# Decay factors of two chunked mixers: masked differences of running sums by two products in the short float32 format, in place of one full float32 product

## The chip, the cores and the metric

The kernel runs on one core of one Trainium2 chip. The metric is the device time of one execution in microseconds (us); the median of the timed runs counts. TensorE (PE in the views, its weight loads are PEld) multiplies, VectorE (DVE) and ScalarE (ACT) work on tiles of 128 partitions, GpSimd (POOL) does a few powers, and SyncE (SP) issues the transfers.

## The reference, cut to what matters

Two layers, each of a SwiGLU feed-forward half step, a token mixer and a second feed-forward half step, on 256 tokens of 1024 features. The mixer runs three groups of heads side by side: differential attention, Mamba-2 (8 heads) and gated DeltaNet (4 heads). The last two need, for every head and every pair of tokens of a block, the factor by which a state decays between them:

```
def segsum_exp(a_cs):
    l = a_cs.shape[-1]
    tril = jnp.tril(jnp.ones((l, l), dtype=bool))
    diff = a_cs[..., :, None] - a_cs[..., None, :]
    return jnp.where(tril, jnp.exp(jnp.where(tril, diff, 0.0)), 0.0)
```

`a_cs` is the running sum of the log decays of a head. There are 12 heads and two blocks of 128 tokens, so 24 tables of 128 x 128 numbers in each layer.

## The kernel before, in words

Every large product is made in float32r, a float32 that the matrix engine multiplies in a shorter format. An operand is split into a high part (the ScalarE cast of line 250) and the rest (the VectorE subtraction of line 251), and three products replace one. Weights come in units of 128 x 1024 numbers; `load` brings them into a ring of 5 buffers, `split` splits them into rings of 7, and `job` (lines 301 to 364) multiplies: lines 327, 342, 343 and 345 for the first matrices and the input projection, lines 238, 239, 241 and 245 for the second matrices and the output projection. Small products, among them those of the decays, are full float32 and go through the helper `mm` (line 389). A full float32 product leaves two matmul records in the trace, a transpose (line 260) or a float32r product one.

In the mixer stage the input projection's units go on while "chains" (generators) turn its results into the three mixers: after each job, `step` advances those chains whose due time, in a clock that the program counts up by hand, has come. The order in which the generator emits instructions is only a first order: when the program is built, a scheduler puts each engine's queue in order by its own estimate of when operands are ready, so that instructions of a chain can stand between two products of one job.

`decays` (line 555) is such a chain. From the gate columns it computes `a12`, the log decays of 12 heads and two blocks (128 x 24), the running sums by two products with triangular constants (`csps`, lines 593 to 595), and then for each of three groups of four heads and each block: a VectorE product `ar` (line 605) of the log decays with the triangle `UT`, a full float32 product of 512 columns with the triangle `SL` (`dps`, line 613), and the exponential (`ex`, line 614). For the first group, which DeltaNet uses, line 618 multiplies the result by `UT` to clear the part above the diagonal; the Mamba groups are masked later through `CB`. The results go out as `E`: `delta` reads `E 0` in line 693 (`LA`), `after_m11` reads `E 1` and `E 2` in line 927.

Other chains that share the queues in this stretch: the attention's `aps`, `dops`, `do`, `dsq`, `dss`, `rsq` and the transposes `mTps` of its result; DeltaNet's `ssps`, the power `r` on GpSimd (line 660), `laps` and `LA`, and the triangular inverse (`gps`, `ups`); the convolutions `conv` of ScalarE and VectorE (lines 516 to 540). Small PSUM results share four banks (`aux`).

Of the kernel before, what the change touches and what calls it, by code (L numbers as in the profile page):

```python
# [10 lines left out]
F32 = mybir.dt.float32  # L11
F32R = mybir.dt.float32r
# [28 lines left out]
LEVELS = (2, 4, 8, 16, 32)  # L41
C_COS = C_LV + 32 * len(LEVELS)
C_SEL = C_COS + 2 * 16
C_N = C_SEL + 2

# [19 lines left out]
def constants():  # L67

    c = np.zeros((P, C_N), np.float32)
    i = np.arange(P)  # L70
    c[:, C_ID : C_ID + P] = np.eye(P)
    c[:, C_UT : C_UT + P] = i[:, None] <= i[None, :]
    c[:, C_SL : C_SL + P] = i[:, None] > i[None, :]

    r, q = i[:, None] % 64, np.arange(64)[None, :]
    c[:, C_M1 : C_M1 + 64] = -1.0 * ((r + 1 == q) & (r % 2 == 0))
    c[:, C_I64 : C_I64 + 64] = r == q
    for n, s in enumerate(LEVELS):
        cols = q[:, (q[0] // s) % 2 == 0]
        c[:, C_LV + 32 * n : C_LV + 32 * (n + 1)] = ((r // s) % 2 == 1) & (r // (2 * s) == cols // (2 * s))  # L80
    freq = np.float32(500000.0) ** (-np.arange(0, 8, 2, dtype=np.float32) / np.float32(8))
    ang = np.arange(SEQ, dtype=np.float32)[:, None] * freq[None, :]
    cos, sin = np.cos(ang), np.sin(ang)
    for b in range(2):
        r = slice(b * P, (b + 1) * P)
        at = C_COS + 16 * b
        c[:, at : at + 16] = np.concatenate([cos[r], cos[r], -sin[r], sin[r]], 1)
    c[:, C_SEL : C_SEL + 2] = i[:, None] // 64 == np.arange(2)[None, :]
    return c


class Kernel:
# [76 lines left out]
    def setup_late(self):  # L169

        nc, a = self.nc, self.a
        c = self.const
        nc.sync.dma_start(self.cst[:, P:], a["cst"][:, P:])
        yield 2

        def bc(name, n, *aps):
            t = c.tile([P, n], F32, name=name)
            at = 0
            for ap in aps:
                nc.sync.dma_start(t[:, at : at + ap.shape[0]], ap.partition_broadcast(P))  # L180
                at += ap.shape[0]
            return t

        self.bias12, self.nA, self.mD, self.nlam = ([] for _ in range(4))
        rows = c.tile([P, P], F32, name="convrows")

        nrows = c.tile([P, P], F32, name="normrows")
        nc.vector.memset(nrows, 0.0)
        for l in range(L):
            r0 = 64 * l  # L190
            nc.sync.dma_start(rows[r0 : r0 + 32], a["m_conv_w"][l].rearrange("k (t c) -> (k t) c", c=P))
            nc.sync.dma_start(rows[r0 + 32 : r0 + 40], a["m_conv_b"][l].rearrange("(t c) -> t c", c=P))
            nc.sync.dma_start(rows[r0 + 40 : r0 + 64], a["g_conv_w"][l].rearrange("k (t c) -> (k t) c", c=P))
            yield 2
            self.bias12.append(bc(f"bias12_{l}", 12, a["g_dt_bias"][l], a["m_dt_bias"][l]))
            self.nA.append(bc(f"nA_{l}", 12, a["g_A_log"][l], a["m_A_log"][l]))
            yield 2
            self.mD.append(bc(f"mD_{l}", 8, a["m_D"][l]))
            r0 = 6 * l
            nc.sync.dma_start(nrows[r0 : r0 + 4], a["m_norm_w"][l].rearrange("(t c) -> t c", c=P))  # L200
            for n, w in enumerate(("g_norm_w", "da_subln_w")):
                r = nrows[r0 + 4 + n : r0 + 5 + n]
                nc.sync.dma_start(r[:, 0:64], a[w][l : l + 1])
                nc.sync.dma_start(r[:, 64:P], a[w][l : l + 1])
            yield 2
        lp = bc("lamp", L * 4 * 32, a["da_lambda"].rearrange("l a b -> (l a b)"))
        lp = lp.rearrange("p (l a b) -> p l a b", l=L, a=4)
        yield 12
        ps = self.aux(0, "cwps")
        nc.tensor.transpose(ps[:, :P], rows, self.ident)  # L210
        nc.tensor.transpose(ps[:, P : 2 * P], nrows, self.ident)
        self.cw = c.tile([P, P], F32, name="cw")
        nc.vector.tensor_copy(self.cw, ps[:, :P])
        self.nw = c.tile([P, 6 * L], F32, name="nw")
        nc.vector.tensor_copy(self.nw, ps[:, P : P + 6 * L])
        for l in range(L):
            nc.scalar.activation(self.nA[l], self.nA[l], AF.Exp)
            nc.vector.tensor_scalar(self.nA[l], self.nA[l], -1.0, None, op0=ALU.mult)
            w = self.nw[:, 6 * l + 5 : 6 * l + 6]
            nc.vector.tensor_scalar(w, w, 1.0 - lambda_init(l), None, op0=ALU.mult)  # L220
            pr = self.s(0, 2, "lsum")
            for m in range(2):
                q = self.h(0, [32], "lq")
                nc.vector.tensor_mul(q, lp[:, l, 2 * m, :], lp[:, l, 2 * m + 1, :])
                nc.vector.tensor_reduce(pr[:, m : m + 1], q, axis=AX.X, op=ALU.add)
            e = self.s(0, 2, "lexp")
            nc.scalar.activation(e, pr, AF.Exp)
            lam = c.tile([P, 1], F32, name=f"lam_{l}")
            nc.vector.tensor_sub(lam, e[:, 0:1], e[:, 1:2])
            nc.vector.tensor_scalar(lam, lam, lambda_init(l), None, op0=ALU.add)  # L230
            self.nlam.append(lam)
# [323 lines left out]
    def decays(self, l, hv):  # L555

        nc = self.nc
        ve = nc.vector
        stt = ve.scalar_tensor_tensor
        two = lambda t: t.rearrange("p (b n) -> p b n", b=2)  # L560

        be = self.s(0, 8, "be")
        nc.scalar.activation(two(be), hv[:, :, 0:4], AF.Exp, scale=-1.0)
        u = self.s(0, 24, "u")
        ve.tensor_tensor(two(u), hv[:, :, 4:16], self.bias12[l].unsqueeze(1).to_broadcast([P, 2, 12]), op=ALU.add)
        e = self.s(0, 24, "e")
        nc.scalar.activation(e, u, AF.Abs)
        nc.scalar.activation(e, e, AF.Exp, scale=-1.0)
        ve.tensor_scalar(be, be, 1.0, None, op0=ALU.add)
        beta = self.s(0, 8, "beta")  # L570
        ve.reciprocal(beta, be)
        yield 0.5

        d = self.s(0, 24, "d")
        ve.tensor_scalar(d, e, 2.0, None, op0=ALU.add)
        ve.reciprocal(d, d)
        z = self.s(0, 24, "z")
        ve.tensor_mul(z, e, d)
        z2 = self.s(0, 24, "z2")
        ve.tensor_mul(z2, z, z)  # L580
        q = self.s(0, 24, "q")
        ve.tensor_scalar(q, z2, 1.0 / 17.0, None, op0=ALU.mult)
        for k in (15.0, 13.0, 11.0, 9.0, 7.0, 5.0, 3.0):
            stt(q, in0=q, scalar=1.0 / k, in1=z2, op0=ALU.add, op1=ALU.mult)
        stt(q, in0=q, scalar=1.0, in1=z, op0=ALU.add, op1=ALU.mult)
        ve.tensor_scalar(u, u, 0.0, None, op0=ALU.max)
        sp = self.s(0, 24, "sp")
        stt(sp, in0=q, scalar=2.0, in1=u, op0=ALU.mult, op1=ALU.add)
        a12 = self.s(0, 24, "a12")
        ve.tensor_tensor(two(a12), two(sp), self.nA[l].unsqueeze(1).to_broadcast([P, 2, 12]), op=ALU.mult)  # L590
        yield 7

        ps = self.aux(0, "csps")
        self.mm(ps[:, 0:24], lhsT=self.UT, rhs=a12)
        self.mm(ps[:, 24:48], lhsT=self.SL, rhs=a12)
        ecs = self.s(0, 48, "ecs")
        nc.scalar.activation(ecs, ps[:, 0:48], AF.Exp)
        self.mx.update(beta=beta, dt=two(sp)[:, :, 4:12], ecs=two(ecs[:, 0:24]), erev=two(ecs[:, 24:48]))

        for n in range(3):  # L600
            ex = self.big([2, 4, P], "ex")
            for b in range(2):
                r = self.w([4, P], "ar")
                at = 12 * b + 4 * n
                ve.tensor_tensor(
                    r,
                    a12[:, at : at + 4].unsqueeze(2).to_broadcast([P, 4, P]),
                    self.UT.unsqueeze(1).to_broadcast([P, 4, P]),
                    op=ALU.mult,
                )  # L610
                yield 0.7
                pd = self.aux(b, "dps")
                self.mm(pd, lhsT=self.SL, rhs=r.rearrange("p h l -> p (h l)"))
                nc.scalar.activation(ex[:, b].rearrange("p h l -> p (h l)"), pd, AF.Exp)
            yield 0.6
            if n == 0:
                e8 = ex.rearrange("p b h l -> p (b h) l")
                ve.tensor_tensor(e8, e8, self.UT.unsqueeze(1).to_broadcast([P, 8, P]), op=ALU.mult)
            self.mx["E", n] = ex

    def after_v(self, l, ps):
# [655 lines left out]
```

## Time and profile before

| what | value |
|---|---|
| timed runs | 1081.48, 1086.86, 1087.26 us; median 1086.86 us |
| profiled execution | 1085.23 us, span 1083.5 us, mean granted TensorE clock 0.991 |
| busy share of the span | PE 98%, PEld 83%, DVE 70%, ACT 56%, POOL 3% |
| data moved | 184.34 MB, mean 170 GB/s |

The span runs from the first to the last instruction; what lies around it in the profiled execution is 1.7 us. Times in rows are from the span's start. Layer 1's mixer stage lies at about 200 to 357 us, layer 2's at about 735 to 887 us. A matmul's recorded duration is longer than its share of the engine, since matmuls are pipelined: how fast they go is read from the starts of successive ones, or from the chain that ended last, which lists the advance.

### The profile page before, as it was taken

What the parts mean: (1) busy time and instruction counts of PE and PEld (TensorE: products, weight loads), DVE (VectorE), ACT (ScalarE), POOL (GpSimd) and SP (SyncE); (2) the same over time, 40 slices, a digit from 0 to 9 for tenths busy, and PEclk for the clock granted to TensorE, in tenths of its full rate; (3) what the DMA queues carried; (4) which work ended last, traced back from release to release, by engine and by line L of the source; (5) the groups of instructions that cost most, each with busy time, mean ns of one, the idle gap of its engine ahead of it and who ended that gap; (6) DMA issues with size and microseconds to landing.
All of it is one profiled execution on the core that took longest, in us unless ns stands there. A gap on an engine that the chain in (4) does not pass through costs nothing.

```text
span 1083.5 us, 17613 instructions
## 1 busy us (share of the span) xinstructions
PE 1056.8 (98%) x6354; PEld 898.4 (83%) x6354; DVE 754.7 (70%) x1550; ACT 605.2 (56%) x1292; POOL 32.0 (3%) x29
## 2 busy tenths in 40 slices
PE   8999999999999999999999999999989999999996
PEld 7888888787987788888878888887878878888885
DVE  5777754886776877774587777457967787777644
ACT  6687643487434566664356666446863445666540
POOL 0000000001001000000000000000010010000000
PEclk9999999998999999999999999999999999999999
DMA  9967664653234676666477666646512449666641
GB/s 274 294 180 208 191 192 143 176 157 97 60 105 145 199 216 190 195 189 195 142 222 211 190 194 191 191 105 194 177 47 72 145 132 264 181 183 187 194 136 39
DMA packets 221551, 184.34 MB, mean 170 GB/s; under 512 B 14608, under 2 KB 201368, under 8 KB 221464
## 3 DMA queue, kind: packets, MB, share of 16 engines
q1 hardware_dynamic: 221464, 183.22, 57.7%
q8 instruction: 50, 0.82, 0.3%
q14 instruction: 37, 0.30, 0.1%
HBM read 182.13 MB, written 1.05 MB: 169 GB/s over the span
## 4 chain that ended last, share of the span: by engine, by line
PE 85%; DVE 8%; issue 2%; DMA 2%; ACT 2%; POOL 1%; SPq 0%; DVEq 0%; POOLq 0%; ACTq 0%
PE ps L327 43%; PE po L238 7%; PE po L239 7%; PE po L245 7%; PE ps L345 4%; PE ps L343 4%; PE ps L342 4%; DVE wl L251 3%; DMA raw<-in_ffn_w_gu_dram 1%; PE ups L389 1%; PE gps L389 1%; POOL rsq L430 1%; PE xps L260 1%; PE yps L389 1%; PE vnps L389 1%
## 5 line engine op out<-in xcount | busy, mean ns | idle before, releaser
L251 DVE TENSOR_TENSOR wl<-raw,wh 128x512 fp32r<-128x512 f32 (+1 forms) x672 | 436.3, 681 | 195.2 <-ACT wh L250 188.4
L250 ACT CAST wh<-raw 128x512 fp32r<-128x512 f32 (+1 forms) x672 | 386.4, 616 | 206.7 <-PE po L245 100.8
L327 PE MATMUL ps<-xT,wh 128*128 128x512 f32 (+1 forms) x1600 | 492.2, 367 | 0.0
L327 PE MATMUL ps<-xT,wl 128*128 128x256 f32 x1376 | 390.5, 284 | 0.0
L327 PEld LDWEIGHTS ps<-xT,wh 128*128 128x128 f32 x1600 | 288.9, 190 | 52.9 <-issue 2.8
L327 PEld LDWEIGHTS ps<-xT,wl 128*128 128x128 f32 x1376 | 261.8, 190 | 4.0 <-issue 3.7
L238 PE MATMUL po<-wh,hT 128*128 128x512 f32 x352 | 137.7, 391 | 0.0
L239 PE MATMUL po<-wl,hT 128*128 128x512 f32 x352 | 137.0, 389 | 0.0
L245 PE MATMUL po<-wh,hT 128*128 128x512 f32 x336 | 103.6, 389 | 0.0
L342 PE MATMUL ps<-wh,xT 128*128 128x512 f32 (+2 forms) x256 | 95.2, 377 | 2.3 <-ACT wh L250 2.2
L343 PE MATMUL ps<-wl,xT 128*128 128x512 f32 (+2 forms) x256 | 94.0, 374 | 0.0
L238 PEld LDWEIGHTS po<-wh,hT 128*128 128x128 f32 x352 | 66.1, 188 | 14.5 <-DVE hh L498 1.0
L239 PEld LDWEIGHTS po<-wl,hT 128*128 128x128 f32 x352 | 66.1, 188 | 13.4
L345 PE MATMUL ps<-wh,xT 128*128 128x512 f32 (+2 forms) x256 | 73.2, 371 | 1.2 <-DVE xT L251 1.2
L245 PEld LDWEIGHTS po<-wh,hT 128*128 128x128 f32 x336 | 63.1, 188 | 13.3
L250 ACT CAST hT<-hh 128x256 fp32r<-128x256 f32 x72 | 29.3, 407 | 70.3 <-DVE hh L500 70.3
L342 PEld LDWEIGHTS ps<-wh,xT 128*128 128x128 f32 x256 | 48.6, 190 | 11.2 <-ACT wh L250 2.6
L343 PEld LDWEIGHTS ps<-wl,xT 128*128 128x128 f32 x256 | 48.4, 189 | 8.3 <-DVE wl L251 0.7
L430 POOL TENSOR_TENSOR rsq<-rs,neghalf 128x1 f32<-128x1 f32 (+2 forms) x20 | 23.8, 1192 | 995.2 <-DVE rs L428 995.2
L345 PEld LDWEIGHTS ps<-wh,xT 128*128 128x128 f32 x256 | 45.0, 188 | 9.5 <-DVE xT L251 2.1
L499 ACT ACTIVATE ga<-ga 128x256 f32<-128x256 f32 x72 | 30.1, 419 | 35.8 <-DVE ga L496 35.8
L251 DVE TENSOR_TENSOR hT<-hh,hT 128x256 fp32r<-128x256 f32 x72 | 30.5, 424 | 26.0 <-ACT hT L250 26.0
(233 smaller groups left out, 925.6 us busy)
## 6 DMA issues: line engine op xcount, KB each, us to landing
raw<-in_ffn_w_gu_dram SPq DMA_DIRECT2D x350, 256.0 KB
raw<-in_ffn_w_down_dram SPq DMA_DIRECT2D x88, 512.0 KB
raw<-in_w_in_dram SPq DMA_DIRECT2D x40, 512.0 KB
raw<-in_w_out_dram SPq DMA_DIRECT2D x16, 512.0 KB
raw<-in_w_in_dram SPq DMA_DIRECT2D x24, 256.0 KB
g<-in_ln_g_dram SPq DMA_DIRECT2D x6, 512.0 KB
b<-in_ln_b_dram SPq DMA_DIRECT2D x6, 512.0 KB
x<-in_x_dram SPq DMA_DIRECT2D x4, 256.0 KB
```

What stands on the lines that cost most here:

```text
L238: mm(p, lhsT=xh, rhs=wh, start=start, stop=False)
L239: mm(p, lhsT=xh, rhs=wl, start=False, stop=False)
L245: mm(p, lhsT=xl, rhs=wh, start=False, stop=False)
L250: self.nc.scalar.copy(hi, src)
L251: self.nc.vector.tensor_tensor(lo, src, hi.bitcast(F32), op=ALU.subtract)
L327: self.nc.tensor.matmul(to, lhsT=a, rhs=r, start=first and n == 0, stop=end and n == len(mms) - 1, skip_group_check=True,)
L342: mm(ps, lhsT=x(kk)[:, 0], rhs=wh[:, s], start=u["part"] == 0 and kk == 0, stop=False)
L343: mm(ps, lhsT=x(kk)[:, 0], rhs=wl[:, s], start=False, stop=False)
L345: mm(ps, lhsT=x(kk)[:, 1], rhs=wh[:, s], start=False, stop=last and kk == ks - 1)
L389: self.nc.tensor.matmul(out, lhsT=lhsT, rhs=rhs, start=start, stop=stop)
L430: nc.gpsimd.tensor_tensor(r, t, self.neghalf[:, :n], op=ALU.pow)
L499: nc.scalar.activation(a, a, AF.Silu)
```

## The change

`a12` becomes four copies side by side, padded to 32 columns each (`a4`, 128 x 128). One more full float32 product of 128 columns, `pT`, gives the running sums with the heads on partitions: the same 24 rows in each of four bands of 32 partitions. The bands are turned into two stationary and moving operands: `hi` is the sum rounded to float32r, the rest is the sum less `hi`; `csm` holds in its bands `hi`, the rest, ones, ones, and `css` holds ones, ones, minus `hi`, minus the rest. For each group and block, `ar` is now `csm` times the columns of a constant that selects the head (`C_IND`), rounded to float32r, and the product of `css` with it is the difference of two running sums in two parts. A second product of 512 columns adds a mask, -1e30 above the diagonal, by an identity in float32r and a constant `below` that is read four times over by a step of zero; the exponential then gives zero there, and line 618's multiplication is gone. The constants grow by 152 columns (part of the second load of `cst`), and the setup casts three 128 x 128 constants and fills two tiles.

```
-        a12 = self.s(0, 24, "a12")
-        ve.tensor_tensor(two(a12), two(sp), self.nA[l].unsqueeze(1).to_broadcast([P, 2, 12]), op=ALU.mult)
+        a4 = self.a4
+        four = [P, 4, 2, 12]
+        ve.tensor_tensor(
+            a4[:, :, 0:24].rearrange("p c (b n) -> p c b n", b=2),
+            two(sp).unsqueeze(1).to_broadcast(four),
+            self.nA[l].unsqueeze(1).unsqueeze(1).to_broadcast(four),
+            op=ALU.mult,
+        )
+        a12 = a4[:, 0, 0:24]
         yield 7
         ps = self.aux(0, "csps")
         self.mm(ps[:, 0:24], lhsT=self.UT, rhs=a12)
         self.mm(ps[:, 24:48], lhsT=self.SL, rhs=a12)
+        pT = ps[:, P : 2 * P]
+        self.mm(pT, lhsT=a4.rearrange("p c n -> p (c n)"), rhs=self.UT)
...
+        hi = self.h(0, [P], "cshi", F32R)
+        nc.scalar.copy(hi, pT)
+        hf = hi.bitcast(F32)
+        nc.scalar.copy(self.csm[0:32], hf[0:32])
+        ve.tensor_tensor(self.csm[32:64], pT[32:64], hf[32:64], op=ALU.subtract)
+        nc.scalar.activation(self.css[64:96], hf[64:96], AF.Copy, scale=-1.0)
+        ve.tensor_tensor(self.css[96:P], hf[96:P], pT[96:P], op=ALU.subtract)
+        yield 0.8
+        below = self.below.unsqueeze(1).to_broadcast([P, 4, P])
         for n in range(3):
             ex = self.big([2, 4, P], "ex")
             for b in range(2):
-                r = self.w([4, P], "ar")
-                at = 12 * b + 4 * n
+                r = self.w([4, P], "ar", F32R)
+                at = C_IND + 12 * b + 4 * n
                 ve.tensor_tensor(
                     r,
-                    a12[:, at : at + 4].unsqueeze(2).to_broadcast([P, 4, P]),
-                    self.UT.unsqueeze(1).to_broadcast([P, 4, P]),
+                    self.csm.unsqueeze(1).to_broadcast([P, 4, P]),
+                    self.cst[:, at : at + 4].unsqueeze(2).to_broadcast([P, 4, P]),
                     op=ALU.mult,
                 )
                 yield 0.7
                 pd = self.aux(b, "dps")
-                self.mm(pd, lhsT=self.SL, rhs=r.rearrange("p h l -> p (h l)"))
+                nc.tensor.matmul(pd, lhsT=self.css, rhs=r.rearrange("p h l -> p (h l)"), start=True, stop=False)
+                nc.tensor.matmul(
+                    pd.rearrange("p (h l) -> p h l", h=4), lhsT=self.identr, rhs=below, start=False, stop=True
+                )
+                self.clock += 0.45
                 nc.scalar.activation(ex[:, b].rearrange("p h l -> p (h l)"), pd, AF.Exp)
             yield 0.6
-            if n == 0:
-                e8 = ex.rearrange("p b h l -> p (b h) l")
-                ve.tensor_tensor(e8, e8, self.UT.unsqueeze(1).to_broadcast([P, 8, P]), op=ALU.mult)
```

## Rows read from the trace of the kernel before

**Rows 1.** The page, busy time, share of the span and count by engine.

```profile
PE 1056.8 (98%) x6354; PEld 898.4 (83%) x6354; DVE 754.7 (70%) x1550; ACT 605.2 (56%) x1292; POOL 32.0 (3%) x29
```

**Rows 2.** Waits of PE: us in total, times, longest.

```profile
PE laps L389 <- DVE LA L693: 3.7, 2, 2.4
...
PE mTps L260 <- DVE do L1081: 1.2, 2, 0.6
```

**Rows 3.** Chain that ended last, layer 1: start us, advance us, what.

```profile
239.23 0.36 PE csps L389 x4
...
242.05 0.86 PE dps L389 x2
...
248.11 0.37 ACT do L1070
...
253.47 0.42 DVE do L1081
...
254.03 0.41 PE mTps L260 x2
...
268.48 11.73 PE ps L327 x80
280.21 1.05 PE gps L389 x32
...
293.13 0.23 PE ps L343
...
299.13 1.31 PE cbps L389 x8
```

**Rows 4.** The same chain, layer 2.

```profile
772.56 0.36 PE csps L389 x4
...
800.88 9.79 PE ps L327 x80
810.67 1.05 PE gps L389 x32
```

**Rows 5.** Timeline of PE in layer 1: start us, us, engine, line, what.

```profile
238.95 0.28 PE L327 MATMUL ps<-xT,wh 128*128 128x256 f32 x1
239.07 0.52 PE L389 MATMUL csps<-a,cst 128*128 128x24 f32 x4
239.43 0.36 PE L327 MATMUL ps<-xT,wh 128*128 128x256 f32 x1
...
247.91 1.08 PE L389 MATMUL dps<-ar,cst 128*128 128x512 f32 x2
```

**Rows 6.** Groups by form, DVE and ACT: busy us, mean ns, idle before.

```profile
L605 DVE TENSOR_TENSOR ar<-a,cst 128x512 f32<-128x512 f32 x12 | 8.2, 686 | 0.0
L743 DVE TENSOR_TENSOR oS<-rps,ecs 128x128 f32<-128x128 f32 x2 | 0.5, 282 | 0.0
L775 ACT COPY S<-sps 128x128 f32<-128x128 f32 x2 | 0.5, 266 | 1.9 <-PE sps L389 1.9
```

**Rows 7.** Tile `ex`: duration ns min/median/max, first and last start us, form.

```profile
L693 DVE SCALAR_TENSOR_TENSOR LA<-laps,d,ex x16: 478/480/482, 264.9 to 803.1; 128x256 f32<-128x256 f32 x16
L614 ACT ACTIVATE ex<-dps x12: 597/598/615, 245.2 to 794.7; 128x512 f32<-128x512 f32 x12
L618 DVE TENSOR_TENSOR ex<-ex,cst x2: 1224/1225/1226, 246.8 to 780.1; 128x1024 f32<-128x1024 f32 x2
```

**Rows 8.** Timeline of ACT in layer 1, while the first `dps` are due.

```profile
239.86 1.28 ACT L540 ACT_TABLE_LOAD   x1
```

**Rows 9.** Windows: stretch, busy us (count) by engine, granted clock, DMA share, GB/s.

```profile
240.00:250.00 10.00, 10.00 (x71) 8.27 (x69) 9.13 (x18) 9.32 (x17) 0.00 (x0) 1.00 0.58 187
...
262.00:264.00 2.00, 2.00 (x10) 1.64 (x9) 0.00 (x0) 0.57 (x2) 2.00 (x1) 0.66 0.00 0
264.00:266.00 2.00, 1.09 (x6) 0.80 (x4) 1.56 (x8) 2.00 (x5) 0.41 (x1) 0.50 0.00 0
...
797.00:799.00 2.00, 0.39 (x4) 0.19 (x2) 1.21 (x7) 2.00 (x6) 0.75 (x1) 1.00 0.00 0
```

More of the change, by code (lines that the diff above doesn't have):

```diff
@@ L43 @@
 C_SEL = C_COS + 2 * 16
-C_N = C_SEL + 2
+C_IND = C_SEL + 2
+C_MB = C_IND + 24
+C_N = C_MB + P
 WIN = (
@@ L88, in constants @@
     c[:, C_SEL : C_SEL + 2] = i[:, None] // 64 == np.arange(2)[None, :]
+    c[:, C_IND : C_IND + 24] = i[:, None] % 32 == np.arange(24)[None, :]
+    c[:, C_MB : C_MB + P] = np.where(i[None, :] < i[:, None], -1e30, 0.0)
     return c
@@ L211, in setup_late @@
         nc.tensor.transpose(ps[:, P : 2 * P], nrows, self.ident)
+        self.a4 = c.tile([P, 4, 32], F32, name="a4")
+        nc.vector.memset(self.a4, 0.0)
+        self.csm = c.tile([P, P], F32, name="csm")
+        nc.vector.memset(self.csm, 1.0)
+        self.css = c.tile([P, P], F32R, name="css")
+        nc.scalar.copy(self.css, self.csm)
+        self.identr = c.tile([P, P], F32R, name="identr")
+        nc.scalar.copy(self.identr, self.ident)
+        self.below = c.tile([P, P], F32R, name="below")
+        nc.scalar.copy(self.below, self.cst[:, C_MB : C_MB + P])
         self.cw = c.tile([P, P], F32, name="cw")
```

## The prediction

> **What bounds the kernel now.** I read the page first, then PE's waits, then the chain that ended last through both mixer stages, the timelines around the decays, and the windows for the clock. PE is busy 98% of the span, the other engines 70% or less [rows 1]. In the whole run PE's recorded waits on the other engines are a few microseconds, the largest 3.7 us before `laps`, in two places [rows 2]. So PE's queue sets the time, and a microsecond less on it counts, unless it lies in front of a wait that would then grow. The chain shows where that is: in layer 1 it runs on PE from `csps` at 239.23 us through the first `dps`, leaves it at 248.11 us for the attention's `do` on ScalarE, VectorE and GpSimd, and comes back with `mTps` at 254.03 us [rows 3]. Between these two PE works at other things and then waits 0.6 us for `do` [rows 2]; two of the layer's six `dps` products stand in that stretch, the first starting at 247.91 us [rows 5].
>
> **Products removed.** One `dps` advances the chain by 0.86 us [rows 3]; there are six in a layer, 12 in all (24 records): 12 x 0.86 = 10.3 us.
>
> **Products added.** Twenty-four float32r products of 512 columns, 12 with `css` and 12 with the mask. The trace has many products of that format and width: one advances the chain by 0.23 us, its weight load included [rows 3]. 24 x 0.23 = 5.5 us. A mask read four times over by a step of zero does not occur before. Its price lies between 0.23 us and that of a full float32 record, 0.86 / 2 = 0.43 us; the instruction is nearest to the first, the same format and width, so I take 0.23. At 0.43 the sum would be 12 x 0.20 = 2.4 us worse.
>
> The Trainium skill, "TensorE: Matmul & The Clock Gate", section "Back-to-back issue gap", gives some 131 ns for a 512-column product in a sustained stream; by it, as an estimate, the 24 products would take 3.1 us and the change would give 2.4 us more. The row above disagrees, and the row decides.
>
> `pT` is one more full float32 product of 128 columns in each layer. `cbps`, two such products of 256 columns and two of 128, takes 1.31 us [rows 3], so 128 columns cost 1.31 / 6 = 0.22 us, and both layers 0.44 us.
>
> Sum on PE: 10.3 - 5.5 - 0.4 = 4.4 us less.
>
> **What the queue order makes of it.** In each layer four of the six `dps` lie on PE's own stretches; the saving there (0.86 - 0.46 = 0.40 us each) less `pT` is 1.6 - 0.2 = 1.4 us, 2.8 us for both layers. The other two save 0.8 us a layer in front of the wait for `do`. With the order as it is, that wait grows by as much and the 0.8 us is lost. But the queue is put in order when the program is built: `csps` stands between two products of one job [rows 5], so the builder moves other products up into a gap that it foresees. If it does so here, the full 4.4 us stays. I take the middle, 3.6 us, and keep 2.8 and 4.4 as ends.
>
> **VectorE and ScalarE.** Line 618 goes: 2 x 1.22 = 2.4 us less on VectorE [rows 7]. Added in each layer are two subtractions on 32 partitions of 128 numbers and a wider `a4`. The nearest row is 0.28 us for 128 numbers on 128 partitions [rows 6]; below nothing and above twice that can't be excluded, but at three times 0.28 a layer VectorE still ends with 0.7 us less in both layers. `ar` keeps its size and so its 0.69 us [rows 6]. ScalarE gains three copies a layer, `hi` and two of 32 partitions, at 0.27 us by the copy of 128 numbers [rows 6], 1.6 us in all, and three casts once in the setup, 0.8 us. All of this is hidden by PE's work; in the stretch from 240 to 250 us, though, VectorE is busy 9.1 of 10 us and ScalarE 9.3 [rows 9], so there the cover is thin (rival 3). The setup's casts and the 78 KB more of constants (152 columns of 128 floats) fall into the first feed-forward stage, without PE waits; as a bound, 78 KB at the mean 170 GB/s is 0.5 us, and I take nothing.
>
> **The longer way to the first exponential.** Before, `ar` needed only `a12`. Now `pT` (0.22), `hi` (0.27), and then, on each of two engines, two pieces (0.55) come first: about 1.0 us, plus what is queued before them. Who waits? `E 0` is read by `LA` from 264.9 us, while `ex` starts at 245.2 us and line 618 at 246.8 us, ending at 248.0 [rows 7]: 17 us of slack, of which line 618 gives back 1.2. The Mamba groups are read later still. So only PE itself can be held up, by a `dps` that heads its queue before `ar` is there. The bank of `csps` is held until the subtractions are done, about a microsecond longer; there are three others. Both cost nothing as long as the input projection's products fill in, which they do now before `dps`: from the end of `csps` to the first one the queue has 242.05 - 239.59 = 2.5 us, filled by them [rows 3]. Without that cover the price is the wait itself.
>
> **The clock.** In layer 1 the granted clock is 0.66 in the window from 262 us and 0.50 in the next, after a stretch of narrow `ssps` and half-height `laps` products and while PE begins to run short; in layer 2 the same stretch, with PE busy only 0.39 of 2 us, keeps 1.00 [rows 9]. The same 80 products take 11.73 us in layer 1 and 9.79 in layer 2 [rows 3, 4]. From `csps` to the first `gps` layer 1 takes 280.21 - 239.23 = 40.98 us, layer 2 810.67 - 772.56 = 38.11: one such fall to the lower of the two levels, 1.2 GHz, costs 2.9 us. The profiled execution, 1085.23 us (span 1083.5 and 1.7 around it), has one fall. I read the timed runs by it, as an estimate: 1085.2 - 2.9 = 1082.3 is near the fastest (1081.48), 1085.2 + 2.9 = 1088.1 near the other two (1086.86, 1087.26). So the median seems to have two falls, and is 1.6 us above the profiled execution.
>
> **The rivals.**
> 1. *Kept, clock as before.* From the profiled execution 1085.2 - 3.6 = 1081.6 us, from the median 1086.9 - 3.6 = 1083.3. I forecast between, 1082.8, and 1081.5 to 1085 as this case's own range. Chance 0.47.
> 2. *Kept, and fewer falls in the median run.* Whether the clock falls differs between layers with the same instructions, so a shifted timing may avoid it: 1083.3 - 2.9 = 1080.4 with one less, 1077.5 with two less. Against it: nothing in the change widens the narrow products before the fall. Chance 0.27.
> 3. *Slower: PE held at the first `dps`.* Place: the new pieces on ScalarE and VectorE between `pT` and `ar`, behind loaded queues. ScalarE has a table load of 1.28 us just there [rows 8], and a piece behind it comes at least that late. The 2.5 us of filling cover that. To be slower by 0.5% (5.4 us, about what a measurement of this kernel can tell) PE must lose 5.4 + 3.6 = 9.0 us, 4.5 us in each layer: the chain would have to be late by 2.5 + 4.5 = 7.0 us. It would give 1092 us or more. Against it: the builder knows the dependence and can put `dps` later. Chance 0.08.
> 4. *The saving is eaten.* PE's wait for `do` and the wait before `laps` grow by what the products save, since both end with work of VectorE and GpSimd: 1086 us, and with the mask at 0.43 us also no better. Chance 0.12.
> 5. *More falls of the clock.* The shorter products leave a thinner PE stretch before 262 us, and the clock falls in both layers in the median run, or stays low longer: one fall more than in the forecast, 1082.8 + 2.9 = 1085.7. For it speaks the fall in layer 1, against it layer 2, which sat idle for more of its window and kept 1.00. Chance 0.06.
>
> The Trainium skill, "TensorE: Matmul & The Clock Gate", section "Part 1: The HAM clock gate", says that the throttled state is the default and that activity releases it; by that rule rival 5 is the one to fear, as the change takes activity away. The trace agrees in layer 1 and not in layer 2 (0.50 and 1.00 above).
>
> **How the numbers follow.** Faster than 1081.4 us: nearly all of case 2 and a fifth of case 1, 0.26 + 0.10 = 0.36. Slower than 1092.3: case 3, 0.08. Within 0.5%: the rest, 0.56. The range runs from 1077.3 (case 2 with two falls less) to 1088 (case 4, and a run with falls that saves only the lower bound); outside it remain case 3 and the edges, some 0.15.
>
> **What the next profile would show.** `dps` with 24 records of some 0.39 us each that advance the chain by 0.23, and `csps` with 0.22 us more. Line 618 gone, and `E 0` still there well before `LA`. If the step with the mask is wrong, its records will advance by more than 0.23 us. If the step on the order is wrong, PE's wait at `mTps` for `do` will be 1.4 us instead of 0.6. For rival 3 there would be a wait of PE or PEld at `dps` for `ar`; for 2 and 5, a granted clock of 1.00, or 0.50, in the windows before `gps` of either layer. A PE queue in another order around `laps` and `ssps` would upset all of this.

## The result

The changed kernel takes 1073.65 us (median, 1073.48 to 1074.08) beside 1086.69 us before: a ratio of 0.989, 95% interval 0.987 to 0.991. That is 13 us faster where the prediction said 3.9, and below its range (1077.3 to 1088.0). Over all the runs below the changed kernel ran 18 times and the kernel before 95 times: means of 1072.69 and 1084.75 us, 12.1 us apart. The profiled execution took 1073.73 us, its span 1071.9.

The page of the changed kernel (busy us, share, count) answers to [rows 1]: PE's busy time is 10.6 us less, the other engines' nearly the same. PE's waits (us in all, times, longest) answer to [rows 2]: the wait for `do`, 1.2 us before, is nearly gone; the one for `LA` is a little longer.

```profile
PE 1046.2 (98%) x6358; PEld 894.5 (83%) x6358; DVE 754.8 (70%) x1554; ACT 606.6 (57%) x1301; POOL 30.6 (3%) x29
```

```profile
PE laps L404 <- DVE LA L728: 4.3, 2, 2.1
...
PE mTps L275 <- DVE do L1116: 0.2, 1, 0.2
```

The new products, on PE's timeline of the changed kernel in layer 1 (start us, us, what): each starts 0.23 us after the one before it, the product with the mask (line 648) like the other. A record lasts 0.39 us because neighbours overlap; the advance is what counts.

```profile
241.73 0.39 PE L647 MATMUL dps<-ar,css 128*128 128x512 f32 x1
241.96 0.39 PE L648 MATMUL dps<-below,identr 128*128 128x512 f32 x1
242.18 2.04 PE L404 MATMUL dops<-dv,aT 128*128 128x64 f32 x16
...
244.35 0.39 PE L648 MATMUL dps<-below,identr 128*128 128x512 f32 x1
244.58 0.39 PE L647 MATMUL dps<-ar,css 128*128 128x512 f32 x1
244.81 0.39 PE L648 MATMUL dps<-below,identr 128*128 128x512 f32 x1
```

The chain that ended last, layer 1 of the changed kernel (start, advance, what), answers to [rows 3]:

```profile
237.20 0.72 PE csps L404 x6
...
238.16 0.17 ACT cshi L626
...
238.34 0.30 ACT csm L628
...
238.66 0.31 ACT css L630
...
250.32 0.34 DVE do L1116
250.66 0.14 issue
250.80 0.41 PE mTps L275 x2
251.21 0.34 PE ssps L404 x4
251.55 0.63 PE laps L404 x4
252.18 1.73 PE ps L342 x13
253.91 0.63 PE laps L404 x4
254.54 1.44 PE ssps L404 x12
255.99 0.02 issue
256.01 0.19 DVE ss L693
256.20 0.07 issue
256.27 2.91 POOL r L695
...
260.20 0.80 DVE LA L728 x2
260.99 0.04 issue
261.04 2.00 PE laps L404 x8
263.04 8.45 PE ps L342 x63
271.49 1.05 PE gps L404 x32
```

From `csps` to the first `gps` it is 271.49 - 237.20 = 34.3 us, before 41.0. Two things are to be seen. PE's queue has another order: no `dps` between `mTps` and `laps`, the `laps` products in rows of four and eight. And a chain that PE waits for shows itself: last `ssps`, `ss`, the power on GpSimd, `d`, `LA`, second `laps`. PE does have `ps` products in it, but not enough to fill it.

The clock, in windows of the changed kernel (stretch, busy us by engine, granted clock, DMA share, GB/s), beside [rows 9]: there is still a fall to 1.2 GHz in each layer, after the windows in which PE waits for `LA`, but in layer 1 it is over by 265 us, where in the profile before it went on into the window from 272 us (0.78).

```profile
258.00:260.00 2.00, 0.90 (x8) 0.69 (x6) 0.80 (x5) 1.99 (x5) 1.17 (x1) 1.00 0.00 0
260.00:262.00 2.00, 0.96 (x6) 0.82 (x8) 2.00 (x8) 2.00 (x6) 0.00 (x0) 0.79 0.00 0
262.00:264.00 2.00, 2.00 (x11) 1.35 (x8) 1.18 (x4) 0.58 (x2) 0.00 (x0) 0.50 0.00 0
264.00:266.00 2.00, 2.00 (x16) 2.00 (x16) 2.00 (x5) 1.14 (x2) 0.00 (x0) 0.85 0.00 0
...
790.00:792.00 2.00, 2.00 (x11) 1.27 (x10) 1.52 (x7) 1.30 (x3) 0.00 (x0) 0.56 0.00 0
```

### The profile page after: what moved, and what is told of

Its sections match the earlier page's. It is cut to its first block, busy times and chain, and to the rows that moved or that the text cites. A ratio compares the mean times of both kernels' runs of the same rounds, so it can differ in the third digit from the quotient of the medians.

```text
span 1071.9 us, 17626 instructions
## 1 busy us (share of the span) xinstructions
PE 1046.2 (98%) x6358; PEld 894.5 (83%) x6358; DVE 754.8 (70%) x1554; ACT 606.6 (57%) x1301; POOL 30.6 (3%) x29
## 4 chain that ended last, share of the span: by engine, by line
PE 84%; DVE 7%; ACT 4%; DMA 2%; issue 2%; POOL 1%; SPq 0%; DVEq 0%; POOLq 0%; ACTq 0%
PE ps L342 43%; PE po L253 7%; PE po L254 7%; PE po L260 7%; PE ps L360 4%; PE ps L357 4%; PE ps L358 4%; DVE wl L266 3%; DMA raw<-in_ffn_w_gu_dram 2%; PE ups L404 1%; PE gps L404 1%; ACT wh L265 1%; PE xps L275 1%; PE yps L404 1%; PE vnps L404 1%
```

## The experiments

The table has, from each profile, the length of the mixer stage (start of the first `csps` to start of the next `xps`) in layers 1 and 2, with a + where the clock fell in it for some 3 us and ++ where for 7 to 14; when the last `ssps` ended after that `csps`, and the start of `LA`, both in layer 2; and the mean granted clock over all timed runs of the kernel. Ratios are to the kernel before on the same chip, with 95% intervals.

| kernel | median us | ratio | stage 1, 2 (us) | last ssps, LA | clock |
|---|---|---|---|---|---|
| before (profile shown ahead) | 1086.69 | 1 | 116.4++, 113.5 | 22.1, 25.8 | 0.992 (95 runs) |
| before_again | 1084.41 | 1.001 [0.999, 1.003] | 115.0+, 116.4++ | 22.1, 25.8 | 0.992 |
| after | 1073.65 | 0.989 [0.987, 0.991] | 110.4+, 110.3+ | 18.9, 23.0 | 0.995 |
| after_again | 1072.82 | 0.992 [0.989, 0.995] | 110.4+, 109.3 | 18.9, 23.0 | 0.995 |
| after_third | 1072.11 | 0.990 [0.987, 0.992] | 110.4+, 109.4 | 18.9, 23.0 | 0.996 |
| after_5 | 1071.75 | 0.988 [0.986, 0.990] | 110.3+, 109.4 | 18.9, 23.0 | 0.997 |
| clock_of_before | 1080.57 | 0.996 [0.994, 0.998] | 113.4+, 113.3+ | 23.2, 26.9 | 0.992 |
| no_pause | 1077.65 | 0.992 [0.990, 0.995] | 111.6+, 113.0++ | 19.8, 23.5 | 0.992 |
| order_of_after | 1083.31 | 0.999 [0.997, 1.002] | 114.0+, 114.0+ | 23.2, 27.0 | 0.992 |
| before_laps_later | 1085.50 | 1.000 [0.998, 1.003] | 115.6++, 114.4+ | 22.1, 25.8 | 0.993 |
| css_full32 | 1076.32 | 0.994 [0.993, 0.996] | 111.7, 111.6 | 17.2, 21.0 | 0.997 |
| one_short | 1078.86 | 0.996 [0.994, 0.998] | 111.5++, 113.0++ | 23.1, 26.9 | 0.991 |
| dps_later | 1074.13 | 0.990 [0.987, 0.993] | 112.1++, 110.5+ | 19.8, 25.2 | 0.996 |
| count_108 | 1073.44 | 0.989 [0.987, 0.990] | 110.1, 110.1 | 19.4, 23.7 | 0.996 |
| pause_2 | 1075.06 | 0.991 [0.989, 0.993] | 110.6, 111.9+ | 20.2, 24.4 | 0.996 |
| mask_thrice | 1074.80 | 0.988 [0.985, 0.990] | 112.6++, 112.6++ | 17.1, 22.2 | 0.994 |
| pow_twice | 1080.88 | 0.998 [0.997, 0.999] | 114.1++, 113.3+ | 18.9, 26.0 | 0.991 |
| before_pow_twice | 1091.49 | 1.008 [1.005, 1.011] | 118.3++, 118.6++ | 22.1, 28.8 | 0.989 |
| ssps_late | 1070.77 | 0.988 [0.986, 0.990] | 109.3, 109.2 | 19.1, 23.2 | 0.997 |
| ssps_late_5 | 1072.12 | 0.988 [0.986, 0.990] | 109.3, 109.2 | 19.1, 23.2 | 0.996 |

**The two kernels again, and the format.** First both kernels once more, and two that change the products only in part.

> The kernel before, unchanged, to see what its executions differ by. Theory C (much of the gain is the clock): the profiled execution before had two falls of TensorE's clock, 3.4 us in the opening and 10.2 us in layer 1's mixer, the changed kernel two of 3.4 us; if falls are chance, the executions of the kernel before spread over 1081 to 1088 us, and the faster ones show a higher mean granted clock (0.995 or more at 1081.5, 0.991 or less at 1085 to 1087). Theory O (the gain is products and queue order): the falls lie at the same places in each execution, and the time stays within 1 us of 1086.7.

> The changed kernel, unchanged. Theory C: another execution may have the fall in the opening too, so that some run lies 2 us or more above 1074. Theory O: 1073.5 to 1074.5 us, no fall in the opening, one of 3.4 us in each mixer.

`css_full32` is the changed kernel with the first product, its operands and its counted cost in full float32:

```
-        self.css = c.tile([P, P], F32R, name="css")
+        self.css = c.tile([P, P], F32, name="css")
-                r = self.w([4, P], "ar", F32R)
+                r = self.w([4, P], "ar")
-                self.clock += 0.45
+                self.clock += 1.08
```

> The changed kernel with the product of the two parts in full float32 again (0.86 us in place of 0.23 us, 12 times), the mask's product, the running sums and everything else as in the change. By the price of the products alone: 12 x 0.63 = 7.6 us more than the change, 1081.3 us. If the price of products is not what decides but the order of the queue around laps and mTps, the order changes too and it lands anywhere from 1076 to 1087; if the wait for do hides a third of it, 1079.

`one_short` is the kernel before with one float32r product for each `dps`; its log decays are rounded to the short format, it has no running sums, no second product, and line 618 stays:

```
-                r = self.w([4, P], "ar")
+                r = self.w([4, P], "ar", F32R)
-                self.mm(pd, lhsT=self.SL, rhs=r.rearrange("p h l -> p (h l)"))
+                nc.tensor.matmul(pd, lhsT=self.SLr, rhs=r.rearrange("p h l -> p (h l)"), start=True, stop=True)
+                self.clock += 0.225
```

> The kernel before with its one product of 512 columns in the short format (log decays rounded to it, so the decays are less exact), no running sums on partitions, no mask product, line 618 kept. PE does 12 x (0.86 - 0.23) = 7.6 us less than before. By the price of the products: 1086.7 - 7.6 = 1079.1 us. If a part of the change's gain comes from something that this edit does not have (line 618 gone, the two parts, the setup's casts in the opening), it stays above the change's 1073.7 us although PE does 3.2 us less than there; if the shorter products alone bring the other queue order, it lies at 1070 to 1072.

Both results speak against products alone. `css_full32` does 12 x (0.86 - 0.23) = 7.6 us more of products than the changed kernel and is 3.5 us slower; it has no wait before the second `laps` and no fall of the clock in its profile, but a wait of 1.7 us a layer at `gps`, for `T` of the triangular inverse. `one_short` does 3.2 us less of products than the changed kernel (12 of 0.23 and `pT`) and is 6.0 us slower, with its last `ssps` 4 us later.

**Price and order apart.** `clock_of_before` leaves all products as changed and gives the builder the old count, without the pause:

```
-        yield 0.8
-                self.clock += 0.45
+                self.clock += 0.853
```

> The changed kernel with the builder's counted cost of a pair of decay products put back to the old 0.853 us and without the pause before the first of them: the same instructions, but a PE order like that of the kernel before (dps pair next to mTps, laps products apart by ps, dops split). Theory of the price (only the cheaper decay products matter): no change against the changed kernel, about 1073 us, mixer stages some 109.3 us each without a fall of the clock. Theory of the order (half of the mixer's gain, about 2.1 us a layer, comes from the order that the builder chose): 3 to 4 us above the changed kernel, 1076.5 to 1078 us, mixer stages 111.4 us each, laps at 0.9 us or more per group of four on average, and the wait of mTps for do back at over 1 us per stage.

PE's order is then nearly that of before (a `dps` pair behind `mTps`, `laps` in twos and fours). It takes 1080.57 us, 4.4 us less than the 1084.93 of the kernel before beside it (95% interval 2.2 to 6.6), at the same mean clock of 0.992. The theory of the price is refuted. The theory of the order gave too little: the time lies 2.6 us above its range, the stages, with a short fall each, 2 us above its 111.4, and only the wait for `do`, at 0.6 us a stage, was put too high. What comes without the new order is thus about what the prediction summed for the products, within a wide interval. Stages with one short fall of the clock can be compared: 113.4 us here, 115.0 in the kernel before (`before_again`, layer 1), 110.4 in the changed kernel. Part of the 3.0 us between the last and the first lies further on: in this kernel the `po` products of a layer are broken into eight pieces instead of four and take 22.0 us instead of 21.1.

`order_of_after` is the mirror: the kernel before with the count of 0.45, 0.213 more for `csps`, and the pause.

```
+        self.clock += 0.213
+        yield 0.8
...
                 self.mm(pd, lhsT=self.SL, rhs=r.rearrange("p h l -> p (h l)"))
+                self.clock += 0.45 - 512 * 4 / 2400
```

> The kernel before with the changed kernel's counted costs (csps 0.213 us dearer, a pause, dps counted at 0.45 us): the old products at their old price, in an order nearer to that of the changed kernel (no dps between mTps and laps, the first laps pairs together). Theory of the price: as the kernel before, 1084 to 1086 us. Theory of the order: 2 to 4 us less, 1080 to 1082 us; mixer stages 112 us instead of 113.6 where the clock stays up, the wait of mTps for do below 1.2 us.

No gain that can be measured (ratio 0.999), against the theory of the order; but the order it got is not that of the changed kernel: the second `laps` stand four and four, one `dps` still stands between the first `laps` and one behind them, and the last `ssps` comes at 23.2 us. With a short fall in both its layer 1 is 0.9 us shorter than that of the kernel before (114.0 and 115.0), and 0.7 of this are the `laps`, which advance PE by 3.4 us instead of 4.05. The counts of the new order, put on the dear products, did not give its order.

> The kernel before with the pause between the two LA blocks counted as 3 us instead of 0.5: the second four laps products stand together instead of two and two, behind 17 ps products instead of 3 and 10. Theory of the order: 0.4 us a layer by the laps that then overlap and about 0.5 us by the shorter wait, 2 us in all, 1082 to 1084 us. Theory of the price: as the kernel before, 1084 to 1086 us.

```
-            yield 0.5
+            yield 3.0 if b == 0 else 0.5
```

No gain either, and no clean test: the wait for `LA` fell into the middle of the eight products, two ahead of it and six behind.

`no_pause` takes a single line out of the changed kernel, `yield 0.8`:

> The changed kernel without the one line that pauses before the first decay product, all else as it is, counted cost included. The earlier run that gave the old counted cost back and took this pause away was 6 to 7 us slower than the changed kernel, but the cost alone leaves the builder's order as it is, so the pause is what decides. Theory of the order (the pause makes the builder put the decay products four and two together and the second eight laps products in one row): without it the second laps stand four and four apart again, 1078 to 1081 us. Rival (the six microseconds were the opening and the clock of that session): 1073 to 1075 us.

1077.65 us: some 4 us slower than the changed kernel, which was not run beside it, just under the range of the theory of the order, and well above the rival's. With it gone the second `laps` are four and four again. (The counted cost matters as well: `clock_of_before` differs from this kernel in nothing else, and there a `dps` stands behind `mTps` and the last `ssps` ends at 23.2 us instead of 19.8.) A pause of 0.8 that stood in no term of the prediction thus carries about a third of the gain; in the stages with one short fall it is 1.2 us a layer (111.6 and 110.4), and the mean clock, 0.992 here, is the other part.

**Filling the gap.** Three kernels move work into PE's wait for `LA`.

`dps_later`, behind the first group:

```
+            if n == 0:
+                self.mx["E", n] = ex
+                yield 2.0
```

> The changed kernel with a pause of 2 us after the first group of decays, so that four dps pairs and 7 more ps products stand nearer to, or in, the gap in which PE waits for LA before the second laps. Theory of the clock (the falls to 1.2 GHz follow that gap): the wait at laps is under 1.5 us instead of 2.4 and the falls after it become rare, 1070 to 1072 us. Rival (the gap and the falls are not linked, and the other dps is only late): 1073 to 1076 us with the falls as before.

> The changed kernel with a pair of decay products counted at 1.08 us instead of 0.45: the same instructions, but ssps and the first laps stand ahead of mTps and 20 ps products behind it, while the eight second laps stay together. In the run with full float32 decay products a like order had no wait before the second laps, no fall of the clock, and was only 3.5 us slower than the changed kernel with 7.6 us more of products. Theory (laps and with them the whole chain of the delta rule come earlier and PE has work while it waits): mixer stages of some 108 us instead of 109.3, 1069 to 1072 us. Rival (PE's total sets the time, the wait only moves): 1072 to 1074 us.

`pause_2` is the same count with `yield 2` for `yield 0.8`.

> As the run with the count of 1.08, and the pause 2 us instead of 0.8: three decay pairs at once, ssps ahead of mTps, and 21 ps products right before the second eight laps. Theory of the chain (it is when the second laps may start, not how PE fills the time before, that counts): 1 to 2 us slower than that run, since two decay pairs and the ssps come later. Rival (the filled gap counts): as that run or up to 2 us faster.

None is faster than the changed kernel: the rivals hold, by which the wait only moves. In `dps_later` the wait before the second `laps` is gone from the list and the time is the same: `LA` starts 2.1 us later, and the clock fell in both layers with no gap ahead of it (PE busy 2.00 of 2 us in each window from 252 to 258 us, and from 780 to 786), which refutes the theory that the falls need the gap. `count_108` has no fall at all in its profile, and the same 1073.4 us. `pause_2` came out 1.6 us slower than `count_108`, as the theory of the chain said; its layer 2 has a short fall that `count_108` has not.

**The chain by itself.** `pow_twice` computes GpSimd's power twice, and PE's queue is the same, instruction by instruction, as in the changed kernel:

```
+        nc.gpsimd.tensor_tensor(r8, ss, self.neghalf, op=ALU.pow)
         nc.gpsimd.tensor_tensor(r8, ss, self.neghalf, op=ALU.pow)
```

> The changed kernel with GpSimd's power (2.90 us between the last ssps and the first LA) computed twice, same PE order, same products. Theory of the chain (in the mixer the time is set by the chain last ssps, ss, power, d, LA, second laps, which PE waits for): 2.9 us more of wait before the second laps in each layer, 5.8 us more in all, 1078 to 1080 us, by falls of the clock after the longer gap perhaps 2 more. Rival (PE's total sets the time, other work fills in): up to 2 us more, 1073 to 1075 us.

> The same doubling in the kernel before, in which the last ssps stands 3.2 us later in the stage and PE waits 1.9 us for LA in each layer. Theory of the chain: 5 to 6 us more than the kernel before. Rival (there the products of PE set the time): up to 2 us more.

> The changed kernel once more, beside the three others on the same chip: 1072.5 to 1074.5 us by both theories.

GpSimd's timeline in layer 1 and PE's first wait in the profile of `pow_twice`:

```profile
256.21 2.90 POOL L695 TENSOR_TENSOR r<-ss,neghalf 128x16 f32<-128x16 f32 x1 [6.54 <-DVE ss L693]
259.19 2.90 POOL L696 TENSOR_TENSOR r<-ss,neghalf 128x16 f32<-128x16 f32 x1
```

```profile
PE laps L404 <- DVE LA L729: 10.2, 2, 5.1
```

Of 2 x 2.9 us on an engine that is busy 3% of the time, PE's wait takes all: 4.3 to 10.2 us. The time grows by 8.8 us (1072.11 to 1080.88), as the theory of the chain said with the falls that it allowed for: with a short fall in both, layer 2 is 3.0 us longer (113.3 and 110.3), and the clock's mean fell from 0.996 to 0.991. The kernel before does the same (10.4 us of wait, 7.7 us slower). So PE's wait for `LA` is paid in full in both kernels.

`mask_thrice` adds the reverse, products without a chain:

```
+                nc.tensor.matmul(
+                    pd.rearrange("p (h l) -> p h l", h=4), lhsT=self.identr, rhs=below, start=False, stop=False
+                )
+                nc.tensor.matmul(
+                    pd.rearrange("p (h l) -> p h l", h=4), lhsT=self.identr, rhs=below, start=False, stop=False
+                )
                 nc.tensor.matmul(
                     pd.rearrange("p (h l) -> p h l", h=4), lhsT=self.identr, rhs=below, start=False, stop=True
                 )
```

> The changed kernel with the product that adds the mask made three times instead of once (masked numbers get -3e30, the others 0, so every decay is the same): 24 more products of 512 columns with the mask read by a step of zero, in nearly the same order. Theory of the price (each costs PE 0.23 us, and PE sets the time): 24 x 0.23 = 5.5 us more, of which the four extra in each layer that stand ahead of the wait before the second laps may be hidden, 2 x 4 x 0.23 = 1.8 us: 3.7 to 5.5 us above the changed kernel's 1073 us, 1076.7 to 1078.5 us. Rival (the step of zero makes it dearer, 0.43 us, and the changed kernel is faster for other reasons): 24 x 0.43 = 10.3 us, 1083 us. Rival (the waits hide the decay products, so that the gain is all order and clock): 1073 to 1074 us.

Between the theories, and below the first one's range: 1074.8 us, some 2 us for 5.5 us of products, and by its ratio none. Two of its four runs, at a mean clock of 0.997, took 1072.1 and 1073.0 us, about 1 us more than the changed kernel's four runs at that clock (1071.3 to 1071.8); the other two, at 0.991, 1076.6 and 1077.1. Its PE no longer waits for `LA`: the products stand where the wait was (the last `ssps` comes 1.8 us earlier, so that its order is not quite that of the changed kernel). That a cheaper decay product would buy little more in the changed kernel is likely by this, and not shown: no run has one.

**The place of ssps, and a better version.**

```
-        yield 5
+        yield 9
         self.spawn(self.delta(l, self.qk, self.sq))
```

> The changed kernel with the pause before the delta rule counted as 9 us instead of 5: the same products, but the last ssps stands behind 20 ps and four decay pairs, so that it ends some 22 us after csps as in the kernel before instead of 18.9. Theory of the chain: the first LA comes some 3 us later in each layer and the stage grows by 1.5 to 3 us of it, 1076 to 1079 us. Rival (the gain over the pure price came from laps that stand together, not from the place of ssps): 1073 to 1075 us.

The edit missed its aim: the last `ssps` ended at 19.1 us. Instead it put all eight first `laps` in a row and shortened the wait to 1.2 us, and was 1.3 us faster than the changed kernel beside it. The same kernel and the changed one once more, side by side:

> The kernel of ssps_late once more, in five rounds. There the count of the pause did not move the last ssps (19.1 us after csps instead of 18.9), but put all eight laps products of each kind in one row and left a wait of 1.2 us instead of 2.1 before the second, with no fall of the clock in any layer. If that is lasting: 1 to 2.5 us below the changed kernel beside it, 1069.5 to 1071.5 us, mean clock 0.997. Rival (chance of that session): the same as the changed kernel, 1072 to 1074 us.

> The changed kernel in five rounds beside it: 1072 to 1074 us, mean clock 0.994 to 0.996, by every theory; it also gives the ratio to the kernel before more closely, 0.988 to 0.991.

1072.12 and 1071.75 us: the rival holds. No version here is faster than the changed kernel.

## Why the prediction was wrong

**The products: right.** In the changed kernel the twelve new products of a layer advance PE by 2.85 us; six old ones by 6 x 0.86 = 5.16 [rows 3]. With `pT` at 0.22 that is 2.1 us a layer, 4.2 in all, for 4.4 predicted; and 4.4 were measured with nearly the old order, if only within 2.2 to 6.6. The step of zero costs nothing (0.23 us, the lower end). This is their price in the rows. It is not what products are worth in every order: `css_full32` pays 3.5 us for 7.6 and `mask_thrice` 1 to 2 for 5.5, and in both PE's wait before the second `laps` is gone.

**What the queue order makes of it: the step that failed.** The prediction let the builder either keep the order and lose 0.8 us a layer, or refill and lose nothing: the ends 2.8 and 4.4. That a new order could itself gain stood in no term; its last sentence only said that another order around `laps` and `ssps` would upset all. What it gained is read from two layers in which the clock did not fall: layer 2 before, 113.5 us, and layer 2 of `after_again`, 109.3. Of the 4.2 us between them the products are 2.1. The `laps` are the largest part of the rest. PE's timeline before, layer 2, with the row behind each:

```profile
788.92 0.70 PE L389 MATMUL laps<-qk 64*128 64x256 f32 x2
789.54 0.39 PE L327 MATMUL ps<-xT,wl 128*128 128x256 f32 x1
...
789.98 0.70 PE L389 MATMUL laps<-qk 64*128 64x256 f32 x2
790.60 1.13 PE L389 MATMUL dps<-ar,cst 128*128 128x512 f32 x2
...
792.25 0.70 PE L389 MATMUL laps<-qk 64*128 64x256 f32 x4
792.88 0.38 PE L327 MATMUL ps<-xT,wh 128*128 128x256 f32 x1
...
794.89 1.13 PE L389 MATMUL laps<-qk 64*128 64x256 f32 x4
795.95 0.39 PE L327 MATMUL ps<-xT,wh 128*128 128x256 f32 x1
...
799.75 1.13 PE L389 MATMUL laps<-qk 64*128 64x256 f32 x4 [2.36 <-DVE LA L693]
800.81 0.39 PE L327 MATMUL ps<-xT,wl 128*128 128x256 f32 x1
```

and in `after_again`, layer 2:

```profile
779.97 0.70 PE L404 MATMUL laps<-qk 64*128 64x256 f32 x4
780.61 0.50 PE L342 MATMUL ps<-xT,wh 128*128 128x256 f32 x2
...
782.34 0.70 PE L404 MATMUL laps<-qk 64*128 64x256 f32 x4
782.97 1.50 PE L404 MATMUL ssps<-cst,sq 128*128 128x2 f32 x12
...
789.54 1.14 PE L404 MATMUL laps<-qk 64*128 64x256 f32 x8 [2.14 <-DVE LA L728]
790.61 0.39 PE L342 MATMUL ps<-xT,wl 128*128 128x256 f32 x1
```

Before, the sixteen records advance PE by 0.62 + 0.62 + 0.63 + 1.06 + 1.06 = 4.0 us, after by 0.64 + 0.63 + 1.07 = 2.3: two records alone cost as much as four in a row, and four as much as eight. That is 1.7 us; the wait for `do`, 0.60 before and 0.17 after, gives 0.4; `aps`, in pairs now, 0.25; `dops` and `ssps` take 0.26 back; the other waits of the stage cancel to 0.1. So 2.1 us a layer, 4.2 in all, are the order's. That it is the order is shown by `clock_of_before` and `no_pause`, which have the changed kernel's products and lose 7 to 8 and some 4 us of its gain; that `laps` are the largest part of it is read from the rows, in `order_of_after` too, and the one kernel meant to test it alone did not.

**The wait for `do`** fell to 0.2 us, neither 0.6 nor 1.4. **VectorE, ScalarE and the longer way** cost next to nothing, as said: `dps` starts 241.73 - 237.04 = 4.7 us after `csps` instead of 2.8, with `ps` and `aps` in between and no wait of PE for `ar` (rival 3), and `LA` still found `E 0` ready. The cover is thinner than the prediction had it, though: the chain that ended last now leaves PE at `csps` and runs over the new pieces on ScalarE (0.17, 0.30 and 0.31 us) to `do`, and PE has to wait 0.2 us for that.

**The clock: right in kind, wrong in size.** Rival 2 came true (and 5 did not), though in the profiles the falls are shorter rather than fewer: the mean granted clock rose from 0.992 in 95 runs to 0.996 in 18. In both sets a run is 0.62 us shorter for each 0.001 of it (a line through the points), so 3.6 of these are 2.2 us. The prediction's price of a fall, 2.9 us, was that of the one long fall; a short one costs 1.0 (110.4 and 109.4 us in `after_third`), or 1.5 in the kernel before (115.0 and 113.5). The prediction left the clock at 0.27 of chance and outside its sum, and named only a shifted timing as its reason. The clock went with the order, not with the products: it stayed at 0.992 with the new products in nearly the old order (`clock_of_before`, `no_pause`) and reached 0.997 with the dear product (`css_full32`). Reading the median as "two falls" was unfounded: the profile itself has a second one that the prediction passed over (0.76 in the window from 8 to 12 us, during the first loads), and of two profiles of the kernel before, both at 1085 us, one had the second fall in layer 2, which kept 1.00 in the other.

**The sum.** Of the 12.1 us between the means the products are 4.2, the order 4.2, the clock 2.2. The clock's part is an estimate from a scattered line. The profiles bear the sum out: the two mixer stages together take 229.9 and 231.4 us in the two profiles of the kernel before, and 220.7, 219.7, 219.8 and 219.7 in the four of the changed one, 10.7 us less on average. Some 1.5 us stay unassigned; they lie outside the mixer stages, where single profiles of one kernel differ by as much (last section). Why the clock falls for a shorter time is open: longer gaps went with a lower clock in `pow_twice`, but `dps_later` fell without one and `count_108` kept 1.00 with one.

The Trainium skill, "TensorE: Matmul & The Clock Gate", section "Back-to-back issue gap", would have given 2.4 us more; the new rows stay at 0.23 us.

## What to carry to other kernels

Where a builder puts the queue in order, price a change twice: in the old order, and in an order that you cannot see. A pause or a counted cost in the diff is an edit of the queue like any other; what it may give is estimated from what narrow products cost in their worst and best places in the rows, and is not zero. PE at 98% busy does not mean that every product counts: here PE waits in one place for a chain over GpSimd, 5.8 us more of which cost 8.8 with the fall of the clock that came along, while 5.5 us more of products cost 1 to 2. Look for the wait, follow it back to the last PE instruction that it starts from, and ask what the change puts ahead of that.

## What the runs showed of the hardware

Half-height products (64 rows) cost by where they stand, not by their count alone: 0.63 us for two or four, 1.06 us for four or eight, in the rows above. By the starts of the single records, in the four that take 0.63 us and the eight that take 1.07 every second one starts 0.01 us after the one before it; in the pairs, and in the fours that take 1.06, none starts sooner than 0.2 us after. And the feed-forward products come at two speeds at the same granted clock of 1.00: in layer 2 the stretch from the first `hTps` to the first `po` of the first feed-forward stage is 662.97 - 548.90 = 114.1 us in the profile of the changed kernel, and 662.63 - 550.39 = 112.2 us in that of `after_again`, with the same instructions. Which of the four such stretches is slow differs from execution to execution. No run here tells why, and 1.8 us of chance in a profile is half of what was predicted for the whole change.
